# Differential attention in a two-layer hybrid backbone: the order of a head pair's key and query projections, and which engine takes which reciprocal root

## The chip, the cores and the metric

The kernel runs on one core of one Trainium2 chip. The metric is the device time of one execution in microseconds (us). Before the change the median of three runs is 1973.07 us (1971.86 to 1974.28); smaller is better.

## What is computed

Two layers of a diffusion backbone work on 256 latent tokens and 256 context tokens, 1024 channels each, in float32. In each layer one input projection feeds three mixers (a recurrence in both directions, latent attention with 16 heads, differential attention with 8 heads); their merged output and a SwiGLU block are added to the stream. The last layer computes outputs, and so queries, for the 256 latent tokens alone. What matters here is the differential attention:

```python
def _rmsnorm(x, g):
    y = xf * lax.rsqrt(jnp.mean(xf * xf, axis=-1, keepdims=True) + EPS)
    return (y * g.astype(jnp.float32)).astype(x.dtype)

def _diff_qk(t, g, rope):                      # queries and keys alike
    u = jnp.moveaxis(t.reshape(B, T, DIFF_HEADS, 2, DIFF_HD), 3, 2)   # two maps of 64 per head
    u = _rmsnorm(u, g)
    return _apply_rope(u, *rope) if rope is not None else u

# in _layer; _attention: out = sum_m mix_w[m] * softmax(scale * q_m k_m^T) v
kd_l, kd_c = _diff_qk(dk, diff_k_g, rope_diff), _diff_qk(dkc, diff_k_g, None)
o_c = _attention(_diff_qk(dq, diff_q_g, rope_diff), concat(kd_l, kd_c), concat(vd_l, vd_c), [1, -lam], DIFF_SCALE)
```

## The kernel before

Arithmetic at float32 precision is made of three passes of a split product: each operand is held as a high and a low half (`split`, L136 to 141), and `mm3` (L199) multiplies high by high, low by high and high by low. Weights arrive as blocks of 128 x 1024 (`wload`, L156): one DMA on SyncE, then ScalarE rounds the high half (`wh`, or `room` for two more buffers in the second layer), and VectorE subtracts it to get the low half (`wl` or `room`). The ring has three blocks in the first layer and five in the second.

**The differential attention** goes through its 8 heads in pairs. `diff_proj(hp)` (L891) is a generator that projects one pair: queries (tiles `ddq`), keys (`ddk`) and values (`dvH`, `dvL`). Each projection is one `gemm_tm` (L449) over two weight blocks; `pst` is its PSUM tile, two token tiles of 128 to a bank. Keys and values always take four token tiles, 96 matmuls of 256 columns; queries take four in the first layer (96 matmuls) and two in the last (48). When two token tiles are ready, `qk_tm` (L892) squares them on ScalarE (`scr`, L894), and on VectorE rotates the latent ones (`rope_tm`, L603: L606, two L610, L616) or multiplies the context ones by the gain (L902), and sums the squares (L904).

**The reciprocal roots** of those sums come from `rsqrt` (L204): three small VectorE operations for a first guess (L210, L213, L214), then three Newton steps. With `soon=True` the steps are nine VectorE operations (L217 to L219), without it twelve GpSimd operations (L222 to L225), one behind the other:

```python
        if soon:
            for _ in range(3):
                V.scalar_tensor_tensor(out=t, in0=y, scalar=-0.5, in1=y, op0=ALU.mult, op1=ALU.mult)
                ...
            return y
        for _ in range(3):
            G.tensor_tensor(out=t, in0=y, in1=y, op=ALU.mult)
            ...
```

Before the change the queries' roots (`drq`) are made on GpSimd and the keys' (`drk`) on VectorE. Keys are multiplied by their root in place (L922, four operations). Queries never are: their root is the scale of the softmax's exponential, and a VectorE operation of one column (L622) and ScalarE's exponential (L623) read `drq`.

**Around it.** `diff_prep(h)` (L934) transposes the head's keys (`dtrk`, L939) and then its queries (`dtrq`, L944) on TensorE and splits them. `diff_sc(h)` computes the two score maps of each query tile in one pair of banks (`S`, L663) and the softmax. `diff_pv(h)` multiplies by the values (`po`, 12 matmuls), transposes the result (`subt`, L992), squares it on ScalarE (L996), takes its root on VectorE (`subr`, again L212 to L219) and scales it (L1000, which reads `subt`). `diff_sub(h)` transposes it back (L1007).

**Two PSUM banks** (`ps_tr`, L95, `bufs=2`) serve all transposes in turn. In the loop over the heads (L1140) a new pair's `dtrq` follows the `subt` of an earlier head by two places, so it takes the bank that L1000 reads.

**What sets the order.** Projections are put on a queue and `fill(ns)` draws matmuls from it between the steps of the attention; `need(hp, dk_)` (L929) draws until the pair is entered in the dictionary `dk_`:

```python
            def need(hp, d):
                while hp not in d:
                    credit[0] = 0.0
                    fill(1)
```

A scheduler then orders each engine's instructions by its own estimate of when they are ready and by priority, the order of the code for most; weight splits go ahead by 90. Every engine runs its instructions strictly in that order.

Of the kernel before, what the change touches and what calls it, by code (L numbers as in the profile page):

```python
# [28 lines left out]
EPS = 1e-6  # L29
# [5 lines left out]
RQ, RK, RDQ, RDK = 0, 32, 64, 128  # L35
NROW = 192

W_RX, W_RG, W_MG, W_DQ, W_DK, W_DV, W_BA, W_BB, W_BC, W_OUT, W_G, W_U = 0, 4, 8, 20, 24, 28, 32, 36, 40, 44, 48, 59
# [25 lines left out]
def tile_hybrid(ctx: ExitStack, tc: tile.TileContext, xt, cvec, cwide, prm, row, dlam, rope, wmod, wmod0, wmodt, wfm, wcq, wckv, wuq, wukv, wlru, wfo, out):  # L64
# [91 lines left out]
    def wload(src, n=1024, now=True):  # L156

        if now and ready:
            key, H, L = ready.popleft()
            assert key == str(src)  # L160
            return H, L
        st = stage()
        nc.sync.dma_start(st[:, :n], src)
        ring["w"] = (ring["w"] + 1) % (WB + len(more["w"]))
        if ring["w"] < WB:
            H = wp.tile([P, 1024], F32R, tag="wh", name="wh")
            L = wp.tile([P, 1024], F32R, tag="wl", name="wl")
        else:
            H, L = more["w"][ring["w"] - WB]
        tc.cur_priority -= first_by[0]  # L170
        parts = split(H[:, :n], L[:, :n], st[:, :n])
        for b, a in zip(parts, hold):
            issue_after(b, a)
        hold.clear()
        low[0] = parts[1]
        tc.cur_priority += first_by[0]
        pace[1] += pace[0]
        while pace[1] >= 1:
            pace[1] -= 1
            slow_step(1)  # L180
        return H, L
# [17 lines left out]
    def mm3(ps, wH, wL, xH, xL, start, stop, skip=False):  # L199
        nc.tensor.matmul(ps, wH, xH, start=start, stop=False, skip_group_check=skip)  # L200
        nc.tensor.matmul(ps, wH, xL, start=False, stop=False, skip_group_check=skip)  # L201
        nc.tensor.matmul(ps, wL, xH, start=False, stop=stop, skip_group_check=skip)  # L202

    def rsqrt(ss, scale, eps, n, name, add=None, soon=False):  # L204

        v = sm.tile([P, n], F32, tag="rqv", name=name + "v", bufs=2)
        t = sm.tile([P, n], F32, tag="rqt", name=name + "t", bufs=2)
        y = sm.tile([P, n], F32, tag="rqy", name=name, bufs=8)
        if add is None:
            V.tensor_scalar(out=v, in0=ss, scalar1=scale, scalar2=eps, op0=ALU.mult, op1=ALU.add)  # L210
        else:
            V.scalar_tensor_tensor(out=v, in0=ss, scalar=scale, in1=add, op0=ALU.mult, op1=ALU.add)  # L212
        V.tensor_scalar(out=y.bitcast(I32), in0=v.bitcast(I32), scalar1=1, scalar2=None, op0=ALU.logical_shift_right)  # L213
        V.tensor_scalar(out=y.bitcast(I32), in0=y.bitcast(I32), scalar1=-1, scalar2=0x5F3759DF, op0=ALU.mult, op1=ALU.add)  # L214
# [3 lines that stand above are left out]
                V.tensor_tensor(out=t, in0=t, in1=v, op=ALU.mult)  # L218
                V.scalar_tensor_tensor(out=y, in0=t, scalar=1.5, in1=y, op0=ALU.add, op1=ALU.mult)  # L219
# [3 lines that stand above are left out]
            G.tensor_tensor(out=t, in0=t, in1=v, op=ALU.mult)  # L223
            G.tensor_scalar(out=t, in0=t, scalar1=-0.5, scalar2=1.5, op0=ALU.mult, op1=ALU.add)
            G.tensor_tensor(out=y, in0=y, in1=t, op=ALU.mult)  # L225
        return y
# [29 lines left out]
    def mm_ns(n):  # L256
        return n / 2.4 + 2.5
# [191 lines left out]
    def gemm_tm(l, widx, xH, xL, toks, ps_, consume):  # L449

        pss = [ps_(f"pst{i}").rearrange("p (t n) -> p t n", t=2) for i in range(len(toks) // 2)]
        for hf in range(2):
            H, L = wload(wfm[l, widx, hf])
            H = H.rearrange("p (k n) -> p k n", n=256)
            L = L.rearrange("p (k n) -> p k n", n=256)
            for i, tt in enumerate(toks):
                for kk in range(4):
                    k = hf * 4 + kk
                    mm3(pss[i // 2][:, i % 2, :], xH[:, k, tt * P:(tt + 1) * P], xL[:, k, tt * P:(tt + 1) * P], H[:, kk, :], L[:, kk, :], k == 0 and i % 2 == 0, k == KT - 1 and i % 2 == 1, True)
                if hf == 1 and i % 2 == 1:  # L460
                    consume(toks[i - 1], pss[i // 2])
                yield 12 * mm_ns(256)
# [80 lines left out]
    for l in range(LAYERS):  # L543
        last = l == LAYERS - 1
        TQ = SEQ if last else T
        qtoks = [0, 1] if last else [0, 1, 2, 3]
        nq = len(qtoks)
# [3 lines left out]
        with ExitStack() as c1:  # L551
# [7 lines left out]
            def t_tok(name):  # L559
                return tk.tile([P, 384], F32, tag="tok", name=name, bufs=8)  # L560
# [7 lines left out]
            def t_v(name, dt=F32R):  # L568
                return tmp("v", 6, dt=dt, name=name)
# [7 lines left out]
            def t_sc():  # L577
                return tmp("sc", 2, name="scr")

            if l == 0:  # L580
# [8 lines left out]
                hH = big.tile([P, KT, T], F32R, tag="big", name="hH")  # L589
                hL = big.tile([P, KT, T], F32R, tag="big", name="hL")  # L590
# [298 lines left out]
            dq_, dk_, drq, dvv, dqk, dpr, dpt, dsub, ds0 = {}, {}, {}, {}, {}, {}, {}, {}, {}  # L889

            def diff_proj(hp):  # L891
                def qk_tm(tt0, ps, ss, store, key, ro):  # L892
                    scr = t_sc()
                    A.activation(scr, ps.rearrange("p t c -> p (t c)"), AF.Square)  # L894
                    for i in range(2):
                        u = t_tok("d" + key)
                        uv = u[:, :256].rearrange("p (h d) -> p h d", d=64)
                        sv_ = ps[:, i, :].rearrange("p (h d) -> p h d", d=64)
                        if tt0 == 0:
                            rope_tm(uv, sv_, tabs[key], i, 4, 64)  # L900
                        else:
                            V.tensor_tensor(out=uv, in0=sv_, in1=rw[:, ro:ro + 64].unsqueeze(1).to_broadcast([P, 4, 64]), op=ALU.mult)  # L902
                        store[tt0 + i] = u
                    V.tensor_reduce(out=ss[:, tt0:tt0 + 2, :], in_=scr.rearrange("p (t h d) -> p t h d", t=2, d=64), axis=AX.X, op=ALU.add)  # L904

                def v_tm(tt0, ps):
                    for hh in range(2):
                        d = [w_[:, tt0 * P:(tt0 + 2) * P].rearrange("p (t c) -> p t c", t=2) for w_ in vv[hh]]
                        split(d[0], d[1], ps[:, :, hh * P:(hh + 1) * P])

                ssq = sm.tile([P, 4, 4], F32, tag="ssq", name="dssq", bufs=2)
                ssk = sm.tile([P, 4, 4], F32, tag="dssk", name="dssk", bufs=2)
                qd, kd = {}, {}
                yield from gemm_tm(l, W_DQ + hp, hH, hL, qtoks, ps_mm, lambda tt0, ps: qk_tm(tt0, ps, ssq, qd, "dq", RDQ))
                rq = rsqrt(ssq[:, :nq, :].rearrange("p a b -> p (a b)"), 1.0, 64 * EPS, nq * 4, "drq")
                drq[hp] = rq.rearrange("p (a b) -> p a b", b=4)
                yield from gemm_tm(l, W_DK + hp, hH, hL, alltoks, ps_mm, lambda tt0, ps: qk_tm(tt0, ps, ssk, kd, "dk", RDK))
                rk = rsqrt(ssk.rearrange("p a b -> p (a b)"), 1.0 / 64, EPS, 16, "drk", soon=True).rearrange("p (a b) -> p a b", b=4)
                yield 1
                for tt in range(4):  # L920
                    uv = kd[tt][:, :256].rearrange("p (h d) -> p h d", d=64)
                    V.tensor_tensor(out=uv, in0=uv, in1=rk[:, tt, :].unsqueeze(2).to_broadcast([P, 4, 64]), op=ALU.mult)  # L922
                dq_[hp], dk_[hp] = qd, kd
                yield 1
                vv = [(t_v("dvH"), t_v("dvL")) for _ in range(2)]
                dvv[hp] = vv
                yield from gemm_tm(l, W_DV + hp, hH, hL, alltoks, ps_mm, v_tm)
# [205 lines left out]
            three_banks(f"pair{l}")  # L1133
            singles[0] = 1
            queue.append(diff_proj(0))
            need(0, dk_)
            run(gemm_fm(l, W_BB, 2, oH, oL, TQ, ps_mm, proj_acc))
# [25 lines left out]
            rk = c1.enter_context(tc.tile_pool(name=f"rk{l}", bufs=1, reuse_waits="tile"))  # L1163
# [112 lines left out]
        with ExitStack() as c1:  # L1276
# [73 lines left out]
            for q in range(2):  # L1350
# [37 lines left out]
                hH = big.tile([P, KT, T], F32R, tag="big", name="hH")  # L1388
                hL = big.tile([P, KT, T], F32R, tag="big", name="hL")
# [106 lines left out]
```

## Time and profile before

| | us |
|---|---|
| three runs, median (lowest to highest) | 1973.07 (1971.86 to 1974.28) |
| the profiled execution, as timed | 1974.12 |
| its span, first to last instruction | 1972.3 |
| TensorE (PE) busy in it | 1930.2 (98%) |
| VectorE (DVE) busy | 1568.3 (80%) |
| ScalarE (ACT) busy | 1069.9 (54%) |
| GpSimd (POOL) busy | 58.8 (3%) |

Rows name a line of the kernel, an engine, and the tile written and read. PEld is TensorE's weight load, which runs beside PE; both wait in TensorE's one stream. In a row of the timeline stand its start in us from the span's start, its length, and in brackets the idle time of its engine just ahead of it with what ended that. Differential attention of the first layer lies between about 258 and 530 us, that of the second between about 1362 and 1600 us. The granted clock of TensorE is at full speed in all of it.

### The profile page before, as it was taken

How to read it: one execution, taken by the hardware profiler on the slowest of the kernel's cores; microseconds unless marked ns; L12 is line 12 of the kernel's file. 1: busy time of each engine (PE TensorE's matmuls, PEld its weight loads, DVE VectorE, ACT ScalarE, POOL GpSimd, SP SyncE). 2: the span in 40 equal slices, each digit the busy share in tenths (PEclk: the TensorE clock that was granted, in tenths of full speed). 3: DMA queues.
4: the chain of work that ended last, by engine and by line, in shares of the span. 5: the costliest groups of instructions: out<-in, count | busy, mean ns of one | idle time of the engine just before them, and what ended most of it. 6: DMA issues, size and time to landing. Idle time of an engine off the chain costs nothing. (4 is left out here: it accounts for less than half of the span.)

```text
span 1972.3 us, 31832 instructions
## 1 busy us (share of the span) xinstructions
PE 1930.2 (98%) x11746; PEld 1666.3 (84%) x11746; DVE 1568.3 (80%) x3838; ACT 1069.9 (54%) x1975; POOL 58.8 (3%) x198
## 2 busy tenths in 40 slices
PE   7999999999999999999999999999999999899999
PEld 4888888988678878888888888988999788898888
DVE  5679965788798888789888876898688889966763
ACT  4568833455576663353233224798444678845552
POOL 0001000000000000000000000012010000000000
PEclk9999999999999999999999999999999999999999
DMA  8311122212234456536656653422322234474553
GB/s 291 99 41 51 53 65 77 76 55 67 70 102 129 140 191 197 184 127 201 196 191 201 200 176 115 151 64 76 128 93 80 65 123 143 156 231 150 185 189 108
DMA packets 91068, 258.16 MB, mean 131 GB/s; under 512 B 10144, under 2 KB 17312, under 8 KB 90656
## 3 DMA queue, kind: packets, MB, share of 16 engines
q1 hardware_dynamic: 90912, 256.13, 39.8%
q8 instruction: 92, 1.51, 0.3%
q14 instruction: 64, 0.52, 0.1%
HBM read 250.85 MB, written 5.24 MB: 130 GB/s over the span
## 5 line engine op out<-in xcount | busy, mean ns | idle before, releaser
L138 ACT ACTIVATE wh<-st 128x1024 fp32r<-128x1024 f32 (+4 forms) x305 | 308.4, 1012 | 367.8 <-PE ps L201 173.1
L138 DVE TENSOR_TENSOR wl<-st,wh 128x1024 fp32r<-128x1024 f32 (+4 forms) x305 | 354.2, 1162 | 125.5 <-ACT wh L138 122.0
L200 PE MATMUL ps<-hH,wh 128*128 128x512 f32 (+1 forms) x504 | 182.0, 361 | 3.8 <-ACT gt L1118 2.9
L202 PE MATMUL ps<-hH,wl 128*128 128x512 f32 (+1 forms) x504 | 180.6, 359 | 1.7 <-DVE wl L138 1.7
L201 PE MATMUL ps<-hL,wh 128*128 128x512 f32 (+1 forms) x504 | 181.3, 360 | 0.0
L200 PE MATMUL pst<-wh,hH 128*128 128x256 f32 x568 | 164.3, 289 | 0.0
L201 PE MATMUL pst<-wl,hH 128*128 128x256 f32 x568 | 162.1, 285 | 0.0
L202 PE MATMUL pst<-wh,hL 128*128 128x256 f32 x568 | 161.9, 285 | 0.0
L200 PE MATMUL ps<-h2H,wh 128*128 128x512 f32 (+1 forms) x368 | 139.1, 381 | 0.7 <-ACT h2H L379 0.7
L201 PE MATMUL ps<-h2L,wh 128*128 128x512 f32 (+1 forms) x368 | 139.5, 380 | 0.0
L202 PE MATMUL ps<-h2H,wl 128*128 128x512 f32 (+1 forms) x368 | 139.5, 380 | 0.0
L621 DVE TENSOR_REDUCE st<-S 128x1 f32<-128x512 f32 (+1 forms) x192 | 113.0, 596 | 21.4 <-ACT dp L623 11.2
L138 DVE TENSOR_TENSOR room<-acc,room 128x1024 fp32r<-128x1024 f32 (+3 forms) x75 | 87.6, 1169 | 30.6 <-ACT room L138 29.1
L200 PEld LDWEIGHTS pst<-wh,hH 128*128 128x128 f32 x568 | 108.6, 191 | 3.8 <-issue 3.3
L200 PEld LDWEIGHTS ps<-hH,wh 128*128 128x128 f32 x504 | 95.3, 189 | 19.3 <-ACT gt L1118 3.9
L202 PEld LDWEIGHTS pst<-wh,hL 128*128 128x128 f32 x568 | 108.5, 191 | 1.7 <-issue 1.4
L201 PEld LDWEIGHTS pst<-wl,hH 128*128 128x128 f32 x568 | 108.6, 191 | 1.1 <-issue 0.7
L202 PEld LDWEIGHTS ps<-hH,wl 128*128 128x128 f32 x504 | 95.2, 189 | 15.6 <-DVE wl L138 2.3
L310 DVE SCALAR_TENSOR_TENSOR ms<-ms,cb 128x512 f32<-128x512 f32 x160 | 107.3, 688 | 1.3
L138 ACT ACTIVATE room<-acc 128x1024 fp32r<-128x1024 f32 (+3 forms) x75 | 76.2, 1017 | 57.6 <-PE ps L201 20.5
L201 PEld LDWEIGHTS ps<-hL,wh 128*128 128x128 f32 x504 | 95.3, 189 | 12.8
L310 DVE SCALAR_TENSOR_TENSOR sq<-ms,cb 128x512 f32<-128x512 f32 x112 | 75.7, 689 | 31.9 <-DMA ms<-wmodt 31.0
(585 smaller groups left out, 5558.3 us busy)
## 6 DMA issues: line engine op xcount, KB each, us to landing
st<-wfm SPq DMA_DIRECT2D x224, 512.0 KB, 3.5
ms<-wmodt SPq DMA_DIRECT2D x160, 256.0 KB, 2.8
acc<-wfm SPq DMA_DIRECT2D x56, 512.0 KB, 3.5
st<-wfo SPq DMA_DIRECT2D x35, 512.0 KB, 3.5
mstage<-wmod SPq DMA_DIRECT2D x16, 512.0 KB, 5.3
acc<-wfo SPq DMA_DIRECT2D x9, 512.0 KB, 3.5
st<-wlru SPq DMA_DIRECT2D x7, 512.0 KB, 3.4
st<-wukv SPq DMA_DIRECT2D x13, 256.0 KB, 2.6
```

The source lines that it names most:

```text
L138: return A.activation(dH, src, AF.Copy), V.tensor_tensor(out=dL, in0=src, in1=f(dH), op=ALU.subtract)
L200: nc.tensor.matmul(ps, wH, xH, start=start, stop=False, skip_group_check=skip)
L201: nc.tensor.matmul(ps, wH, xL, start=False, stop=False, skip_group_check=skip)
L202: nc.tensor.matmul(ps, wL, xH, start=False, stop=stop, skip_group_check=skip)
L310: issue_after(V.scalar_tensor_tensor(out=o, in0=st, scalar=1.0, in1=cb[:, v, :], op0=ALU.mult, op1=ALU.mult, accum_out=sums[:, i - i0, h, ...
L621: V.tensor_reduce(out=st[:, 0:1], in_=S, axis=AX.X, op=ALU.max, negate=True)
```

## The change

Inside `diff_proj` the keys' projection, their root and their multiplication now come first, and the queries' projection and root after them. The keys' root loses `soon=True` and is made on GpSimd; the queries' root gets it and is made on VectorE. The pair is entered in `dq_` and `dk_` after the queries' root, with no `yield` behind it, so that `need` returns only when the first token tile of the values' projection has been issued too. L922 of before is L919 of after.

```diff
                 qd, kd = {}, {}
-                yield from gemm_tm(l, W_DQ + hp, hH, hL, qtoks, ps_mm, lambda tt0, ps: qk_tm(tt0, ps, ssq, qd, "dq", RDQ))
-                rq = rsqrt(ssq[:, :nq, :].rearrange("p a b -> p (a b)"), 1.0, 64 * EPS, nq * 4, "drq")
-                drq[hp] = rq.rearrange("p (a b) -> p a b", b=4)
                 yield from gemm_tm(l, W_DK + hp, hH, hL, alltoks, ps_mm, lambda tt0, ps: qk_tm(tt0, ps, ssk, kd, "dk", RDK))
-                rk = rsqrt(ssk.rearrange("p a b -> p (a b)"), 1.0 / 64, EPS, 16, "drk", soon=True).rearrange("p (a b) -> p a b", b=4)
+                rk = rsqrt(ssk.rearrange("p a b -> p (a b)"), 1.0 / 64, EPS, 16, "drk").rearrange("p (a b) -> p a b", b=4)
                 yield 1
                 for tt in range(4):
                     uv = kd[tt][:, :256].rearrange("p (h d) -> p h d", d=64)
                     V.tensor_tensor(out=uv, in0=uv, in1=rk[:, tt, :].unsqueeze(2).to_broadcast([P, 4, 64]), op=ALU.mult)
+                yield 1
+                yield from gemm_tm(l, W_DQ + hp, hH, hL, qtoks, ps_mm, lambda tt0, ps: qk_tm(tt0, ps, ssq, qd, "dq", RDQ))
+                rq = rsqrt(ssq[:, :nq, :].rearrange("p a b -> p (a b)"), 1.0, 64 * EPS, nq * 4, "drq", soon=True)
+                drq[hp] = rq.rearrange("p (a b) -> p a b", b=4)
                 dq_[hp], dk_[hp] = qd, kd
-                yield 1
                 vv = [(t_v("dvH"), t_v("dvL")) for _ in range(2)]
```

How it moves instructions is shown at two places of the second layer. The first is VectorE at the third head pair (hp = 2), where the last projection of the pair has just ended. Before, the keys' chain and the chain of `subr` run in step, the keys are multiplied, and L1000 follows:

```order
L138 TENSOR_TENSOR room<-acc,room 128x1024 [waits DMAHW6_49,Activation_49]
L210 TENSOR_SCALAR drkv<-dssk 128x16 [waits DVE_49]
L212 SCALAR_TENSOR_TENSOR subrv<-subss,s_16013 128x2 [waits Activation_49,Pool_49]
L213 TENSOR_SCALAR drk<-drkv 128x16 [waits DVE_49]
...
L922 TENSOR_TENSOR ddk<-ddk,drk 128x256 [waits DVE_49]
L922 TENSOR_TENSOR ddk<-ddk,drk 128x256 x3
L1000 TENSOR_TENSOR so<-subt,subr 128x256 [waits DVE_49,PE_49]
```

After, at the same place of VectorE's stream:

```order
L213 TENSOR_SCALAR drk<-drkv 128x16 [waits DVE_49]
L606 TENSOR_TENSOR ddq<-pst_16391,tabdq 128x256 [waits Activation_49]
L214 TENSOR_SCALAR drk<-drk 128x16 [waits DVE_49]
L610 TENSOR_TENSOR rp<-pst_16391,tabdq 128x128 x2
L606 TENSOR_TENSOR ddq<-pst_16391,tabdq 128x256
L616 TENSOR_TENSOR ddq<-ddq,rp 128x256 [waits DVE_49]
L904 TENSOR_REDUCE dssq<-scr 128x8
L919 TENSOR_TENSOR ddk<-ddk,drk 128x256 [waits Pool_49]
L919 TENSOR_TENSOR ddk<-ddk,drk 128x256 x3
...
L212 SCALAR_TENSOR_TENSOR subrv<-subss,s_16013 128x2 [waits Activation_49]
...
L1000 TENSOR_TENSOR so<-subt,subr 128x256 [waits DVE_49,PE_49]
```

L214, the last VectorE step ahead of the GpSimd chain, now stands behind the first rotation of the queries; the keys' multiplication waits for GpSimd (Pool) with only four rows between; and the queries' second rotation, one weight split, both chains and L1000 stand behind it.

The same place on TensorE, the transposes for the first head of that pair (`pst_16519` and `pst_16480` are the values' tile before and after). Before:

```order
L939 MATMUL dtrk<-ident,ddk 128x128 [waits DVE_49] x4
L944 MATMUL dtrq<-ident,ddq 128x128 [waits DVE_49,Activation_49]
L944 MATMUL dtrq<-ident,ddq 128x128
L663 MATMUL S<-dkH,dqH 128x512 x2
L200 MATMUL pst_16519<-wh,hH 128x256
```

After:

```order
L939 MATMUL dtrk<-ident,ddk 128x128 [waits DVE_49] x4
L663 MATMUL S<-dkH,dqH 128x512 x2
L663 MATMUL S<-dkL,dqH 128x512 x2
L663 MATMUL S<-dkH,dqL 128x512 x2
L944 MATMUL dtrq<-ident,ddq 128x128 [waits DVE_49,Activation_49]
L944 MATMUL dtrq<-ident,ddq 128x128
L200 MATMUL pst_16480<-wh,hH 128x256
```

The score matmuls moved ahead of `dtrq`; between the end of the pair's last projection and `dtrk` stand 48 matmuls of values, 12 of `po` and 2 of `subt` both before and after.

The second place is VectorE at the second head pair (hp = 1) of the second layer. Before:

```order
L922 TENSOR_TENSOR ddk<-ddk,drk 128x256 [waits DVE_49]
L922 TENSOR_TENSOR ddk<-ddk,drk 128x256 x3
L138 TENSOR_TENSOR room<-acc,room 128x1024 [waits DMAHW1_49,Activation_49]
L621 TENSOR_REDUCE st_16023<-S 128x1 [waits PE_49]
L138 TENSOR_TENSOR dkL<-dtrk,dkH 128x512 [waits Activation_49]
```

After:

```order
L138 TENSOR_TENSOR wl<-st,wh 128x1024 [waits DMAHW7_49,Activation_49]
L919 TENSOR_TENSOR ddk<-ddk,drk 128x256 [waits Pool_49]
L919 TENSOR_TENSOR ddk<-ddk,drk 128x256 x3
L606 TENSOR_TENSOR ddq<-pst_15834,tabdq 128x256 [waits Activation_49]
...
L138 TENSOR_TENSOR room<-acc,room 128x1024 [waits DMAHW0_49,Activation_49]
L616 TENSOR_TENSOR ddq<-ddq,rp 128x256 [waits DVE_49]
```

The queries' rotations now stand behind the wait for GpSimd, and their last step (L616) behind one more weight split; on TensorE, `dtrk` and `dtrq` come directly behind the 48 matmuls of values here, ahead of the score matmuls.

## Rows read from the trace of the kernel before

**Rows 1.** The page's first part: busy time, share, instructions.
```profile
PE 1930.2 (98%) x11746; PEld 1666.3 (84%) x11746; DVE 1568.3 (80%) x3838; ACT 1069.9 (54%) x1975; POOL 58.8 (3%) x198
```

**Rows 2.** Waits of PEld and PE, whole span: total us, times, longest.
```profile
PEld S L663 <- ACT dp L623: 8.5, 27, 0.7
PEld dtrk L939 <- DVE ddk L922: 2.8, 10, 0.5
...
PE dtrq L944 <- DVE so L1000: 0.4, 1, 0.4
```

**Rows 3.** Timeline of POOL, queries' root of hp 1, first layer.
```profile
351.46 0.21 POOL L222 TENSOR_TENSOR drqt<-drq 128x16 f32<-128x16 f32 x1 [83.04 <-DVE drq L214]
...
352.65 0.22 POOL L222 TENSOR_TENSOR drqt<-drq 128x16 f32<-128x16 f32 x1
...
354.73 1.13 POOL L225 TENSOR_TENSOR drq<-drq,drqt 128x16 f32<-128x16 f32 x1
```

**Rows 4.** Timeline of DVE at the same place.
```profile
354.56 1.22 DVE L138 TENSOR_TENSOR wl<-st,wh 128x1024 fp32r<-128x1024 f32 x1 [3.24 <-ACT wh L138]
```

**Rows 5.** Timeline of PE, hp 2 of the second layer, from the keys' end.
```profile
1480.27 0.28 PE L985 MATMUL po<-pH,dvH 128*128 128x256 f32 x1
...
1481.59 0.28 PE L987 MATMUL po<-pH,dvL 128*128 128x256 f32 x1
...
1487.94 0.60 PE L939 MATMUL dtrk<-ident,ddk 128*128 128x128 f32 x4
1488.38 0.38 PE L944 MATMUL dtrq<-ident,ddq 128*128 128x128 f32 x2
```

**Rows 6.** Timeline of ACT at the same place.
```profile
1480.53 0.60 ACT L894 ACTIVATE scr<-pst 128x512 f32<-128x512 f32 x1 [2.34 <-PE pst L202]
```

**Rows 7.** Timeline of DVE at the same place.
```profile
1480.22 0.48 DVE L610 TENSOR_TENSOR rp<-pst,tabdk 128x128 f32<-128x128 f32 x2
1480.73 0.43 DVE L616 TENSOR_TENSOR ddk<-ddk,rp 128x256 f32<-128x256 f32 x1
...
1482.43 1.21 DVE L138 TENSOR_TENSOR room<-acc,room 128x1024 fp32r<-128x1024 f32 x1
...
1486.08 1.43 DVE L922 TENSOR_TENSOR ddk<-ddk,drk 128x256 f32<-128x256 f32 x4
1487.43 0.42 DVE L1000 TENSOR_TENSOR so<-subt,subr 128x256 f32<-128x256 f32 x1
```

**Rows 8.** Timelines of PE and DVE, hp 3 of the second layer.
```profile
1521.85 0.28 PE L985 MATMUL po<-pH,dvH 128*128 128x256 f32 x1
...
1529.01 0.42 DVE L1000 TENSOR_TENSOR so<-subt,subr 128x256 f32<-128x256 f32 x1
```

**Rows 9.** Timeline of DVE, hp 1 of the second layer.
```profile
1430.44 0.42 DVE L606 TENSOR_TENSOR ddq<-pst,tabdq 128x256 f32<-128x256 f32 x1 [1.20 <-ACT scr L894]
...
1434.04 0.42 DVE L616 TENSOR_TENSOR ddq<-ddq,rp 128x256 f32<-128x256 f32 x1
...
1444.82 0.17 DVE L214 TENSOR_SCALAR drk<-drk 128x16 int32<-128x16 int32 x1
...
1446.91 1.43 DVE L922 TENSOR_TENSOR ddk<-ddk,drk 128x256 f32<-128x256 f32 x4
```

**Rows 10.** Timeline of PE, hp 1 of the second layer.
```profile
1446.98 0.50 PE L663 MATMUL S<-dkH,dqH 64*128 64x512 f32 x2
...
1447.87 0.85 PE L939 MATMUL dtrk<-ident,ddk 128*128 128x128 f32 x4
```

**Rows 11.** Timelines of PE and DVE, hp 3 of the first layer.
```profile
466.55 0.66 PE L992 MATMUL subt<-ident,so 128*128 128x128 f32 x4
...
468.55 0.16 DVE L212 SCALAR_TENSOR_TENSOR subrv<-subss,s 128x4 f32<-128x4 f32 x1 [0.75 <-ACT scr L996]
...
472.60 0.69 DVE L1000 TENSOR_TENSOR so<-subt,subr 128x512 f32<-128x512 f32 x1
...
473.43 0.63 PE L944 MATMUL dtrq<-ident,ddq 128*128 128x128 f32 x4 [0.36 <-DVE so L1000]
```

## The prediction, made before the changed kernel had run

> **What bounds the kernel now.** I read the page's first part first: TensorE is busy for 98% of the span [rows 1], so a change that takes no matmul away and adds none can move the time only through the few per cent in which TensorE stands. The change adds and removes no matmul. Next I read the waits of TensorE's two streams. Two kinds belong to the edited steps: the key transposes wait for the keys' multiplication, 2.8 us in ten places, and one query transpose waits 0.4 us for L1000, which still reads the bank that it wants [rows 2]. The largest kind in the attention, the score matmuls that wait for the exponential ahead of them, is 8.5 us in 27 places [rows 2]. So there are about 3.2 us that the edit can win where it works, and no reserve: whatever makes TensorE stand longer goes into the time nearly whole. Last I read the timelines around the eight head pairs, because VectorE obeys its order strictly and a new wait in its stream delays all that is queued behind.
>
> **What the change removes.** The keys' nine Newton steps on VectorE leave the way from the last key to its transposes, and the four multiplications move ahead of the queries' projection. With that the 2.8 us of waiting for the keys go, and the 0.4 us for L1000 is counted anew below: 3.2 us gained at most. VectorE's own work stays: the queries get the nine steps, with 16 columns in the first layer as the keys had, 8 in the last.
>
> **What it adds: a wait of VectorE for GpSimd, eight times.** The chain on GpSimd has twelve operations. Undisturbed, four of them take 1.19 us (352.65 less 351.46 [rows 3]), so twelve take 3.57 us. The multiplication L919 waits for the last of them, and everything behind it on VectorE waits too. What does that cost? It depends on the place.
>
> At hp 0 and hp 1 of the first layer nothing else is due: VectorE stood idle for 3.24 us at this very spot before [rows 4], and the queries' projection, 96 matmuls, runs meanwhile. I cost these two and hp 0 of the second layer, whose transposes come only after a long projection of another branch, at nothing. If that cover were gone, each would cost 3.57 us.
>
> At hp 2 of the second layer I follow the new order. TensorE issues a 256-column matmul each 0.12 us (eleven steps of `po` in 1.32 us [rows 5]). The pair's last projection ends at the same time as before, about 1480.27 us by the old trace, for the work ahead of it is the same. ScalarE squares that result until 1481.13 [rows 6]; only then may VectorE begin the queries' rotation L606 (0.42 [rows 9]), and L214 (0.17 [rows 9]) stands behind it: 1481.65. Now GpSimd starts. Some operations of VectorE that run beside it read tiles in SBUF as it does, and one such overlap cost dearly before: an operation of GpSimd took 1.13 us against 0.22 while VectorE subtracted a weight half [rows 3, 4]. So the chain lasts from 3.57 us (no overlap) to 4.5 (one such overlap). I take 4.0, between them, as the operations of VectorE that now run beside it are shorter than that weight split: 1485.65. The four L919 occupy 1.35 us until the next start (1487.43 less 1486.08 [rows 7]): 1487.0. The rest of the rotation takes 0.94 (1480.22 to the end of L616 [rows 7]): 1487.95. One weight split and the two small chains took 3.65 us from 1482.43 to 1486.08 [rows 7], of which some 0.2 now run earlier: 1491.4. L1000 takes 0.42 [rows 7]: 1491.8.
>
> When is TensorE there? Before, `dtrk` began at 1487.94 and `dtrq` 0.44 us later [rows 5]. The work ahead of `dtrk` is the same, and it finds its keys ready (1487.0); but the six score matmuls, 0.89 us (1446.98 to 1447.87 [rows 10]), now stand between it and `dtrq`: 1489.3. `dtrq` takes the bank that L1000 reads, so TensorE stands from 1489.3 to 1491.8, **2.5 us** (2.1 to 3.0 with the chain's bounds). Before, L1000 was done at 1487.85, half a microsecond ahead of `dtrq`. At hp 3 the rows repeat to the hundredth (L1000 starts 7.16 us behind the first `po` in both [rows 5, 7, 8]) and the new order is alike: again **2.5**.
>
> The Trainium skill, page "SBUF — State Buffer", section "Who interferes with whom", says that a VectorE instruction with two SBUF inputs and a GpSimd instruction that reads SBUF exclude each other for a whole instruction. By that rule only L616 of the four rows between L214 and L919 (0.43 us in the row above) would hold the chain, so 4.0 us is its ceiling there and 2.5 us the wait's; the rows 3 and 4 show one such exclusion, and its length fits (1.13 us until the weight split's end), but no row shows which operations do not exclude.
>
> At hp 1 of the second layer there is no L1000 in the way; the queries themselves come late. The last projection ends 48 matmuls (5.76 us) ahead of 1446.98 [rows 10], at 1441.22, and the keys' now another 5.76 us earlier, 1435.46. L214 ended 3.77 us after the keys [rows 9, 10]: 1439.23. The chain ends at 1442.8, or at 1443.7 with one overlap, since a weight split now stands between L214 and L919. L919: 1444.2 or 1445.1. The queries' rotation with its weight split took 4.02 us (1430.44 to 1434.46 [rows 9]): 1448.2 or 1449.1. TensorE wants the second `dtrq` at about 1447.4 (1446.98 and the 0.44 of `dtrk`). It stands for 0.8 to 1.7 us; I take **1.3**.
>
> At hp 2 and hp 3 of the first layer the queries have 96 matmuls, so the keys' wait is over early. But `need` now lets 12 matmuls of values go ahead of `po`, and these are missing between `subt` and `dtrq`: 18 remain (2.16 us), with `subt` and `dtrk` (0.44 each) and the scores (0.89) about 4.0 us. VectorE needs 2.0 us from `subt` to `subrv` (466.55 to 468.55), fourteen small operations, nine of which each follow on the last at 0.21 us (ten in 2.09 us [rows 9]), about 2.4 together, and L1000 with 0.69 [rows 11]: 5.1. That makes 1.0 us of standing each; 2.2 if the keys' wait has pushed the queries' rotation back by 1.2 us, my estimate of what remains of the chain's 3.57 when VectorE has done the softmax steps between L214 and L919. I take **1.4** each. The new order has more independent work beside the keys' transposes of hp 1, which I leave at nothing.
>
> **The sum.** 2.5 + 2.5 + 1.3 + 1.4 + 1.4 = 9.1 us added, 3.2 taken: **+5.9 us**. The profiled execution, 1974.12 us (span 1972.3 and 1.8 around it), would become 1980.0; it lies 1.05 us above the median, so the median becomes 1979.0. Lower bound: 2.1 + 2.1 + 0.8 + 1.0 + 1.0 less 3.2 is +3.8, 1976.9. Upper bound: 3.0 + 3.0 + 1.7 + 2.2 + 2.2 and nothing gained is +12.1, 1985.2. A measurement here can tell about 0.2%, 3.9 us, from no change.
>
> **Rivals.** *The standing is paid back* (not slower): while TensorE waits at `dtrq`, ScalarE and VectorE get through the softmax, and the score matmuls behind find their banks free. For it speaks that 8.5 us of such waits exist [rows 2]; against it, that it is VectorE that is late, and it comes out of the wait with the same queue. It decides if over half of the 9.1 us return: 9.1 less 4.3 (half of the 8.5) less 3.2 is +1.6, 1974.7, within 0.2%. Chance 0.27.
>
> *The waits for GpSimd hide everywhere* (faster): if the two banks were not claimed as I read, or TensorE reached `dtrq` later, only the 3.2 us and some of the score waits (a quarter, 2.1) would count: -5.3, 1967.8. For it speaks that three of eight places are idle on VectorE; against it, the 0.4 us for L1000, which shows the bank's claim [rows 2, 11]. Chance 0.09.
>
> *The wait reaches the weights too* (slower still): weight splits are queued behind L919. If at each of the five busy places TensorE also stood for what is left of the chain, 3.57 less the 2 us of rows between, 1.6 each, the sum would be 5.9 + 8 = +13.9, 1987.0. Against it: the ring holds three or five blocks, and a block feeds 2.9 to 5.8 us of matmuls. Chance 0.04.
>
> That the change does not do what it says is not among them: the order shows the keys ahead and L919 waiting for Pool at all eight places.
>
> **How the numbers follow.** The forecast, slower by 3.8 to 12.1 us, has 0.60; with the third rival 0.04. Slower by over 0.2%: 0.64; within: 0.27; faster: 0.09. The likeliest time is 1979.0. The range runs from 1972.0, which leaves out the faster case and a fifth of the paid-back one (its own range is 1970 to 1977), to 1985.5, the upper bound: about 0.18 is left out. The forecast's own range is 1976.9 to 1985.2.
>
> **What would show it.** In the profile after, VectorE's waits must name `ddk` L919 behind GpSimd, some 8 times and 15 us or more in total; TensorE's must name `dtrq` behind `so` L1000, 2 to 3 us at each of two places of the second layer, and about 1 at two of the first; waits of `dtrk` for `ddk` must be gone. GpSimd's chain at hp 2 and 3 of the second layer should begin near 1481.8 and 1523.4. I am wrong if `dtrq` finds its bank free, if the score waits fall by as much as `dtrq` adds, or if TensorE's busy share rises.

## The result, and the profile after

The changed kernel takes 1990.24 us (median of four runs, 1989.12 to 1993.48) against 1973.25 us before: a ratio of 1.0087, 95% interval 1.0075 to 1.0099. It is slower by some 17 us, where 5.9 were forecast and 12.1 was the upper bound.

The page's first part, after (the answer to [rows 1]; the span is 1987.9 us, before 1972.3):

```profile
PE 1934.4 (97%) x11746; PEld 1671.2 (84%) x11746; DVE 1571.6 (79%) x3838; ACT 1070.8 (54%) x1975; POOL 53.5 (3%) x198
```

TensorE ran the same 11746 matmuls. Its busy time rose by 4.2 us, so that some of them ran slower, and its idle time (span less busy) rose from 42.1 to 53.5 us, by 11.4. Together that is the 15.6 us by which the span grew. So there are two losses, and only one of them was in the forecast.

Waits after, whole span (engine, what it waited for, total us, times, longest), which answer to [rows 2]:

```profile
DVE ddk L919 <- POOL drk L225: 20.7, 8, 3.7
...
PEld S L663 <- ACT dp L623: 10.2, 27, 2.1
PE dtrq L944 <- DVE so L1000: 9.9, 4, 2.9
...
PE dtrq L944 <- DVE ddq L616: 1.7, 1, 1.7
```

VectorE waits for GpSimd at eight places. TensorE waits for L1000 at four and for the queries (L616) at one, 11.6 us in all. The key transposes no longer wait for `ddk`. The place in the second layer that was followed step by step (hp = 2), first VectorE, then GpSimd, then TensorE (timelines; compare [rows 5, 7]):

```profile
1492.46 0.17 DVE L214 TENSOR_SCALAR drk<-drk 128x16 int32<-128x16 int32 x1
...
1493.27 0.41 DVE L616 TENSOR_TENSOR ddq<-ddq,rp 128x256 f32<-128x256 f32 x1
...
1496.46 1.43 DVE L919 TENSOR_TENSOR ddk<-ddk,drk 128x256 f32<-128x256 f32 x4 [2.18 <-POOL drk L225]
...
1502.10 0.42 DVE L1000 TENSOR_TENSOR so<-subt,subr 128x256 f32<-128x256 f32 x1
```

```profile
1492.71 0.21 POOL L222 TENSOR_TENSOR drkt<-drk 128x16 f32<-128x16 f32 x1 [41.20 <-DVE drk L214]
...
1493.31 0.43 POOL L224 TENSOR_SCALAR drkt<-drkt 128x16 f32<-128x16 f32 x1
...
1496.20 0.22 POOL L225 TENSOR_TENSOR drk<-drk,drkt 128x16 f32<-128x16 f32 x1
```

```profile
1498.87 0.60 PE L939 MATMUL dtrk<-ident,ddk 128*128 128x128 f32 x4
...
1499.96 0.39 PE L663 MATMUL S<-dkH,dqL 64*128 64x512 f32 x2
1502.67 0.41 PE L944 MATMUL dtrq<-ident,ddq 128*128 128x128 f32 x2 [2.32 <-DVE so L1000]
```

The chain on GpSimd lasts 3.71 us (1492.71 to 1496.42), VectorE stands for 2.18 of it, the rest of the queries' rotation, a weight split, both chains and L1000 come only behind that, and TensorE stands for 2.32 us. All of that is the forecast's mechanism. What the forecast did not have is in the next table: TensorE's granted clock in the first layer at hp = 2 (window, its length, then busy us and instructions of PE, PEld, DVE, ACT and POOL, the granted clock as a share of full speed, and two DMA columns):

```profile
416.00:420.00 4.00, 2.21 (x16) 1.43 (x14) 3.41 (x23) 0.60 (x1) 0.00 (x0) 0.97 0.39 131
420.00:424.00 4.00, 3.48 (x17) 3.51 (x17) 2.77 (x6) 1.67 (x3) 0.00 (x0) 0.50 0.01 2
424.00:428.00 4.00, 4.00 (x26) 4.00 (x26) 2.85 (x6) 3.01 (x7) 0.00 (x0) 0.68 0.00 0
428.00:432.00 4.00, 4.00 (x33) 3.46 (x32) 3.23 (x9) 1.20 (x4) 0.00 (x0) 1.00 0.38 134
```

TensorE stood for 2.3 us up to 420.5. The granted clock then fell to half, 1.2 of 2.4 GHz: in the window from 420, in half a microsecond of which TensorE still stood, 17 matmuls went through, and in the one from 428, at full speed, 33. The transposes there show it in one row (compare [rows 11], the same transposes at hp = 3 before, 0.63 us):

```profile
420.52 1.09 PE L944 MATMUL dtrq<-ident,ddq 128*128 128x128 f32 x4 [2.30 <-DVE so L1000]
```

Such falls stand at four places of the attention after (from about 420, 536, 1457 and 1546 us) and at none before. One window of each of the other three:

```profile
536.00:540.00 4.00, 4.00 (x12) 3.08 (x12) 1.93 (x7) 2.45 (x6) 0.00 (x0) 0.60 0.28 105
1456.00:1460.00 4.00, 3.05 (x13) 2.18 (x14) 3.69 (x15) 0.70 (x2) 0.00 (x0) 0.68 0.41 131
1544.00:1548.00 4.00, 1.67 (x9) 1.50 (x8) 3.90 (x22) 0.84 (x2) 0.00 (x0) 0.77 0.36 131
```

Busy time times the missing share of the clock, summed over windows of 4 us, makes 7.3 us of them; at the end of the kernel, where both kernels have two falls, it is 2.9 against 4.2. The windows show one execution, but the mean granted clock of every run agrees: 0.993 to 0.995 in the four runs of the changed kernel, 0.995 to 0.998 in 53 runs of the kernel before.

### The profile page after: what moved, and what is told of

The parts are those of the page before. It is cut to its first block, busy times and chain, and to the rows that moved or that the text cites. A ratio compares the mean times of both kernels' runs of the same rounds, so it can differ in the third digit from the quotient of the medians.

```text
span 1987.9 us, 31830 instructions
## 1 busy us (share of the span) xinstructions
PE 1934.4 (97%) x11746; PEld 1671.2 (84%) x11746; DVE 1571.6 (79%) x3838; ACT 1070.8 (54%) x1975; POOL 53.5 (3%) x198
## 4 chain that ended last, share of the span: by engine, by line
PE 62%; DVE 12%; ACT 6%; issue 3%; POOL 1%; DMA 0%; POOLq 0%; DVEq 0%; ACTq 0%
PE ps L200 11%; PE ps L201 10%; PE ps L202 10%; PE ps L428 4%; PE po L202 2%; PE po L201 2%; PE po L200 2%; PE pst L200 2%; PE pst L202 2%; PE pst L201 2%; PE ps L429 2%; DVE wl L138 2%; PE ptr L635 2%; PE po L1365 1%; PE S L663 1%
## 5 line engine op out<-in xcount | busy, mean ns | idle before, releaser
L138 ACT ACTIVATE wh<-st 128x1024 fp32r<-128x1024 f32 (+4 forms) x305 | 308.3, 1013 | 360.5 <-PE ps L201 180.5
L138 DVE TENSOR_TENSOR wl<-st,wh 128x1024 fp32r<-128x1024 f32 (+4 forms) x305 | 354.2, 1163 | 122.5 <-ACT wh L138 119.1
L200 PE MATMUL pst<-wh,hH 128*128 128x256 f32 x624 | 181.9, 291 | 0.0
L201 PE MATMUL pst<-wl,hH 128*128 128x256 f32 x624 | 180.0, 289 | 0.0
L202 PE MATMUL pst<-wh,hL 128*128 128x256 f32 x624 | 179.8, 288 | 0.0
L621 DVE TENSOR_REDUCE st<-S 128x1 f32<-128x512 f32 (+1 forms) x192 | 113.0, 597 | 25.4 <-ACT dp L623 14.4
L200 PEld LDWEIGHTS pst<-wh,hH 128*128 128x128 f32 x624 | 120.9, 194 | 3.5 <-issue 3.1
L201 PEld LDWEIGHTS pst<-wl,hH 128*128 128x128 f32 x624 | 120.8, 194 | 2.8 <-issue 2.2
L202 PEld LDWEIGHTS pst<-wh,hL 128*128 128x128 f32 x624 | 120.7, 193 | 2.0 <-issue 1.8
L138 DVE TENSOR_TENSOR room<-acc,room 128x1024 fp32r<-128x1024 f32 (+3 forms) x75 | 87.5, 1168 | 29.3 <-ACT room L138 27.9
L138 ACT ACTIVATE room<-acc 128x1024 fp32r<-128x1024 f32 (+3 forms) x75 | 76.2, 1017 | 59.8 <-PE ps L201 19.4
L623 ACT ACTIVATE dp<-S,st,drq 128x512 f32<-128x512 f32 (+1 forms) x96 | 67.7, 705 | 57.4 <-DVE st L622 37.0
```

Of the source, the lines that this page charges most:

```text
L138: return A.activation(dH, src, AF.Copy), V.tensor_tensor(out=dL, in0=src, in1=f(dH), op=ALU.subtract)
L621: V.tensor_reduce(out=st[:, 0:1], in_=S, axis=AX.X, op=ALU.max, negate=True)
L623: A.activation(dst, S, AF.Exp, scale=sc_ap, bias=st[:, 1:2], accum_out=st[:, 2:3] if total is None else total)
```

## Experiments

Theory A: VectorE's wait for GpSimd makes VectorE late, and TensorE stands for it at `dtrq`. Theory B: the new order of the projections does it. Ratios are against runs of the kernel before that were taken together with the run.

**The order alone.** The new order, both roots on the engines of before:

```diff
-                rk = rsqrt(..., 16, "drk")...
+                rk = rsqrt(..., 16, "drk", soon=True)...
...
-                rq = rsqrt(..., nq * 4, "drq", soon=True)
+                rq = rsqrt(..., nq * 4, "drq")
```

> The new order of the projections, but both reciprocal roots on the engines of before: the keys' on VectorE, the queries' on GpSimd. Theory A (VectorE's wait for GpSimd holds L1000, and TensorE stands at dtrq behind it): the waits of L919 for GpSimd are gone, dtrq waits for so L1000 under 2 us in all instead of 9.9, the granted clock does not fall in the differential attention, and the time is 1968 to 1978 us. Theory B (the order alone does it: queries projected last and twelve matmuls of values drawn ahead make dtrq come before VectorE is done): dtrq still stands 7 us or more in all, 1985 to 1992 us.

Measured: 1975.62 us, ratio 1.0007 (0.9997 to 1.0016). The waits for GpSimd are gone, `dtrq` waits 2.2 us for L1000 (A had put under 2), all of it in the first layer, and the clock does not fall in the attention. The order alone costs nothing that can be measured.

**The engines alone.** The old order with the roots swapped (`soon=True` moved from the keys' root to the queries').

> The old order of the projections, but the roots swapped: keys' on GpSimd, queries' on VectorE. Theory A: the chain of 3.6 us now lies directly between the last keys and their transposes, and VectorE has the chain of subr (about 1.9 us) beside it; VectorE waits some 1.5 to 2 us for GpSimd at each busy place, dtrk waits about 1.5 to 2 us longer for ddk at each of five or six places: 1979 to 1987 us. Theory B: without the new order no more than 2 us are lost, 1972 to 1976 us.

Measured: 1990.03 us, ratio 1.0082 (1.0066 to 1.0097), as slow as the whole change and above what A expected. Here TensorE stands at the key transposes, and the clock fell in the attention too (4.2 us by the same sum). Waits, whole span:

```profile
DVE ddk L922 <- POOL drk L225: 22.1, 8, 3.7
PEld dtrk L939 <- DVE ddk L922: 12.2, 21, 2.4
```

So the loss comes with the engines, in either order, and shows where TensorE next needs VectorE. That speaks for A and against B.

**How long GpSimd takes.** The keys' root with one Newton step, and with six (`steps=1` or `6` in the loop over L222 to L225, for `drk` alone; with one step the root is only a rough one). At the four places where TensorE stood for L1000, its order between `dtrk` and `dtrq` is that of the changed kernel to within one matmul.

> The changed kernel with one Newton step instead of three in the keys' root on GpSimd (four operations, 1.2 us); the keys' root is then only a rough one, as two steps are left out. Theory A: VectorE has other rows for longer than that between L214 and L919 at the busy places, so it waits at most 5 us in all; dtrq waits for so L1000 0 to 3 us in all, the clock does not fall, 1972 to 1979 us. Rival E: over 1985 us.

> The changed kernel with six Newton steps instead of three in the keys' root on GpSimd (24 operations, some 7.1 us; the value is the same to rounding). Theory A: VectorE's wait for GpSimd grows by 3.6 us at each of eight places, to some 49 us; TensorE's standing grows by about 3.6 at each of five places, 18 us, and the clock falls behind each: 2006 to 2016 us. Rival E (the loss is one of order and clock, and hardly depends on the chain's length): under 1998 us.

Measured: 1975.40 us (ratio 1.0003, 0.9994 to 1.0013) and 2014.38 us (1.0196, 1.0181 to 1.0211). With one, three and six steps VectorE waits:

```profile
DVE ddk L919 <- POOL drk L225: 6.6, 8, 1.4
```

```profile
DVE ddk L919 <- POOL drk L225: 43.7, 8, 7.3
```

and 20.7 us between them; A had put at most 5 us with one step and some 49 with six. The loss follows the length of the chain: (1990.24 - 1975.40) / (20.7 - 6.6) and (2014.38 - 1990.24) / (43.7 - 20.7) are each 1.05 us of time for each microsecond that VectorE waits, the clock's part and the harmless places included. The changed kernel was timed apart from the other two; by the ratios the rates are 1.2 and 0.9, so about one. With one step the clock does not fall in the attention, with six it falls at five places there, worth 13.9 us.

**Both roots on VectorE**, in the new order (`soon=True` for the keys too).

> The new order with both roots on VectorE. No operation of VectorE waits for GpSimd in the differential attention; VectorE has nine small operations more for each pair than with the keys' or the queries' root on GpSimd, about 1.9 us. Theory A (what counts is how late VectorE comes to L1000, whatever makes it late): about as late as with the wait of 2.2 us, so dtrq waits for so L1000 6 to 10 us in all and the time is 1983 to 1990 us. Rival D (only the standing wait for another engine costs, since VectorE's own operations are fitted in between): 1974 to 1979 us.

Measured: 1973.14 us, ratio 0.9992 (0.9983 to 1.0002), a little less than D expected. Here A as I had put it was wrong: VectorE has more to do than in the changed kernel (1577.1 us busy against 1571.6), and nothing is lost. The timeline of VectorE at hp = 2 of the second layer shows one reason:

```profile
1481.95 0.17 DVE L217 SCALAR_TENSOR_TENSOR drkt<-drk 128x16 f32<-128x16 f32 x1
1482.04 0.28 DVE L610 TENSOR_TENSOR rp<-pst,tabdq 128x128 f32<-128x128 f32 x1
1482.24 0.17 DVE L218 TENSOR_TENSOR drkt<-drkt,drkv 128x16 f32<-128x16 f32 x1
1482.32 0.28 DVE L610 TENSOR_TENSOR rp<-pst,tabdq 128x128 f32<-128x128 f32 x1
```

Between independent rows a step of the chain takes 0.08 to 0.09 us from start to start. I had counted 0.2 us each, as they take one behind the other. Nine of them cost about 0.8 us, where the wait for GpSimd costs 2.2 at the same place. It also tells that the queries' root on VectorE is not the loss, which leaves the keys' root on GpSimd.

There is a second reason at that place: TensorE's order is not that of the changed kernel. Twelve matmuls of values stand between the scores and `dtrq`, and `dtrq` waits for `dkL`, which reads `dtrk`, and not for L1000, which begins behind it (so it does not take the bank that L1000 reads there):

```profile
1491.72 0.44 PE L944 MATMUL dtrq<-ident,ddq 128*128 128x128 f32 x2 [0.24 <-DVE dkL L138]
...
1492.24 0.42 DVE L1000 TENSOR_TENSOR so<-subt,subr 128x256 f32<-128x256 f32 x1
```

L1000 is even later here than in the changed kernel, 11.5 us behind the end of the pair's last projection (1480.73) against 10.9, and no longer matters. The order and the bank are like that at hp = 3 too, and in the run of the order alone, with eleven matmuls. So in the second layer these two runs change what TensorE asks for as well as what VectorE does, and they do not tell the two apart. In the first layer TensorE's order between `dtrk` and `dtrq` is the same to within one matmul; there `dtrq` waits for L1000 0.75 us at each of two places instead of 2.30 and 2.91. The run with one step, where that order stays in both layers, is the cleaner one.

**Another bank.** `subt` in the single bank of `po` (`ps_sc("subt")`), in the changed kernel and in the kernel before, so that `dtrq` takes no bank that L1000 reads.

> The changed kernel, with the tile subt in the single bank of po in place of the two banks of the transposes, so that dtrq no longer takes a bank that L1000 reads. VectorE still waits for GpSimd about 20 us in all. Theory A: dtrq waits for so L1000 nowhere, the 9.9 us and the falls of the clock behind them go: 1974 to 1981 us. Rival C (VectorE is late, and TensorE meets that at the next tile instead: dtrq behind ddq, the scores behind dqL, po behind L1000): 1985 us or more, with the 9.9 us under other names.

> The kernel before with subt in the bank of po. It tells what the bank is worth without the change. Theory A: only the 0.4 us that dtrq waited for L1000 can go, 1970 to 1975 us. Rival C (po now waits for L1000 of the head before): over 1977 us.

Measured: 1995.37 us (ratio 1.0109, 1.0094 to 1.0124) and 1983.55 us (1.0051, 1.0034 to 1.0068). The other bank costs 8 us by itself, among them 4.3 us that TensorE waits for L1000 ahead of the transposes back. The change still costs 11.8 us on top of it. `dtrq` waits for L1000 nowhere; TensorE's waits have other names:

```profile
PE ptr L635 <- DVE dkL L138: 11.0, 9, 2.4
...
PE dtrq L944 <- DVE ddq L616: 1.7, 1, 1.7
```

A was wrong here and rival C right: the bank is where the lateness shows, and not what makes most of it cost.

**Work drawn ahead**: 24 or 36 matmuls of the projections between `dtrk` and `dtrq` of each new pair.

```diff
                 split(kH, kL, ptk)
+                if h in (2, 4, 6):
+                    fill(3600)
                 ptq = ps_tr("dtrq")
```

> The changed kernel with 24 or 36 matmuls of the projections drawn from the queue between the key and the query transposes of the first head of each new pair (they are taken from later places, none is added). VectorE's wait for GpSimd stays about 20 us. Theory F (TensorE's order has too little work ahead of dtrq for the time that VectorE is late, and that is all of the loss, with the clock behind it): dtrq waits for so L1000 under 2 us in all, the clock does not fall there, 1972 to 1979 us. Rival C (the lateness only shows at the next tile, since the work drawn ahead is missing later): 1984 us or more.

Measured: 1990.38 us, ratio 1.0083 (1.0067 to 1.0099): nothing is won, against theory F. `dtrq` no longer waits for L1000, but other waits of TensorE grow by about as much, and the clock still falls at two places (from about 410 and 471 us, 2.8 us):

```profile
PE S L663 <- ACT dp L623: 9.8, 9, 2.8
PE ptr L635 <- DVE dkL L138: 4.9, 3, 2.4
```

The first was 2.7 us in the changed kernel. Matmuls that fill one gap were missing in the next.

**Filler**: 28 matmuls that nothing reads, ahead of `dtrk` at the five places where TensorE stood.

```diff
                 ptk = ps_tr("dtrk")
+                if h in ((4, 6), (2, 4, 6))[l]:
+                    for _ in range(28):
+                        nc.tensor.matmul(ptk[:, :256], hH[:, 0, :P], hH[:, 0, :256], start=True, stop=True, ...)
```

> The changed kernel with 28 matmuls of 256 columns that nothing reads, put ahead of the key transposes at the five places where TensorE stood: 140 of them, 16.8 us of added work at full speed, in place of 11.6 us of standing. Theory G (the clock fell because TensorE stood): the standing and the four falls of the clock (7.9 us) go: 1990.2 + 16.8 - 11.6 - 7.9 = 1987.5, so 1985 to 1990 us, and the granted clock is 1.0 throughout the attention. Rival H (the clock falls there whether TensorE stands or not): 1993 to 1997 us.

Measured: 1987.81 us, ratio 1.0072 (1.0056 to 1.0088), 16.8 us of added work and yet no slower than the change; the mean granted clock of its four runs is 0.996 to 0.998, as before the change. VectorE waits 20.0 us for GpSimd as before, but where the clock had fallen it is full (windows, same columns):

```profile
420.00:424.00 4.00, 3.84 (x30) 2.88 (x29) 3.14 (x6) 2.47 (x4) 0.00 (x0) 1.00 0.00 2
...
1544.00:1548.00 4.00, 3.70 (x31) 3.06 (x30) 3.60 (x7) 1.82 (x4) 0.00 (x0) 1.00 0.49 157
```

In the changed kernel these two windows are at 0.50 and 0.77. Three of the four falls are gone, those at the places that were filled, so there the clock fell because TensorE stood. The one near 536 us stays (1.6 us), where G had none; a wait of 2.1 us for the gate (`gt` L1121), at no filled place, stands ahead of it.

**The yield put back** behind the entry of the pair, in the changed kernel and in the two orders without the wait for GpSimd:

```diff
                 dq_[hp], dk_[hp] = qd, kd
+                yield 1
```

> The changed kernel with the yield behind the entry of the pair put back, so that the twelve matmuls of values stay between subt and dtrq in the first layer. Theory A with the term for twelve matmuls (1.44 us) as predicted: dtrq's wait for so L1000 in the first layer falls from 5.2 to about 2.3 us, the second layer's 4.6 stays, and the time is 1984 to 1989 us. Rival: the twelve matmuls do not matter, 1989 to 1992 us.

> The new order with the roots on the engines of before (keys' on VectorE, queries' on GpSimd) and the yield put back. Theory F: the 2.2 us that dtrq waited for L1000 in the first layer go: 1969 to 1974 us. Rival: no difference from the order without the yield, 1974 to 1977 us.

> The new order with both roots on VectorE and the yield put back behind the entry of the pair, so that twelve matmuls stay between subt and dtrq in the first layer. Theory F: what dtrq still waited there (1.5 us) goes, and nothing else changes: 1968 to 1973 us. Rival: VectorE's nine more operations for each pair show elsewhere: 1975 us or more.

Measured: 1982.77 us (ratio 1.0044, 1.0031 to 1.0056), 1970.25 us (0.9983, 0.9974 to 0.9993) and 1970.61 us (0.9985, 0.9975 to 0.9995). In the first, `dtrq` waits 2.0 us for L1000 in the first layer instead of 5.2, and of the clock's 4.7 us in that layer 1.3 are left: the missing `yield` was worth some 8 us of the change (7.5 by the times, 8.5 by the ratios), more than expected, since falls of the clock went with the waits. Its eight runs lie between 1980.51 and 1988.31 us, with mean granted clocks from 0.997 down to 0.994, and the trace is of the fastest: how far the clock falls differs from run to run. The two others are faster than the kernel before, by some 3.3 us, about the 3.2 that the forecast had as the gain: keys ahead of queries do help, with the `yield` kept and the keys' root on VectorE.

## Why the prediction was wrong, point by point

**Right.** The direction, the cause and the places. The key transposes no longer wait for `ddk`, VectorE waits for GpSimd at eight places (20.7 us, 15 or more forecast), and at hp 0 and hp 1 of the first layer its waits of 3.7 us are followed by no wait of TensorE. The second layer's three terms were 2.5, 2.5 and 1.3 us; they measure 2.32, 2.33 and 1.66. The steps at hp 2 hold as well: counted from the end of the pair's last projection (1491.24 in the new trace), GpSimd begins after 1.5 us where 1.4 were forecast, TensorE comes to `dtrq` after 9.1 (9.0), and L1000 ends after 11.3 (11.5). The chain's length was put at 4.0 us with 3.57 and 4.5 as bounds and is 3.71 there. The rule of the Trainium skill ("SBUF — State Buffer", section "Who interferes with whom") agrees with these rows: beside L616 (two SBUF inputs, 0.41 us) one GpSimd operation takes 0.43 us in place of 0.20 and ends 0.06 us behind it, and the other eleven are as short as ever.

**Wrong: the sum had no term for the clock.** This is the step that failed. I took each microsecond that TensorE stands as one microsecond lost. Behind four waits in the attention the granted clock fell to half and stayed there for 3 to 6 us, 7.3 us of loss. The section on what bounds the kernel read TensorE's waits but not what a longer one does to the matmuls behind it. Without the clock the measured waits less the gain, 11.6 - 3.2 = 8.4 us, lie inside the forecast's 3.8 to 12.1. The filler shows the cause at three of the four places, 5.7 of the 7.3 us.

**Wrong in size: hp 2 and hp 3 of the first layer**, 1.4 us each, 2.2 at most; they measure 2.30 and 2.91. The base of that term held: it was 1.0 us, and without any wait for GpSimd (the order alone) the two places measure 1.09 and 1.10, with 0.57 us of it (one step) 1.14 and 1.00. Mis-sized is what the wait for GpSimd adds. I put it at 1.2 us at most and took 0.4; VectorE waits 1.86 and 2.19 us there, and `dtrq` waits 1.2 and 1.8 us longer than with the order alone. The lateness shows between `subt` and `subrv`, for which I took the 2.0 us of [rows 11]. After the change nine of the twelve rows of the queries' chain stand ahead of `subrv`, 0.21 us apiece, and VectorE begins them 1.7 us behind `subt`, where with one step it is 0.1:

```profile
415.46 0.17 DVE L210 TENSOR_SCALAR drqv<-dssq 128x16 f32<-128x16 f32 x1
...
416.08 0.18 DVE L217 SCALAR_TENSOR_TENSOR drqt<-drq 128x16 f32<-128x16 f32 x1
416.29 0.17 DVE L218 TENSOR_TENSOR drqt<-drqt,drqv 128x16 f32<-128x16 f32 x1
...
417.22 0.15 DVE L212 SCALAR_TENSOR_TENSOR subrv<-subss,s 128x4 f32<-128x4 f32 x1
```

`subt` began at 413.75, so 3.5 us passed, and 3.75 at hp 3 (472.22 to 475.97); with one step it is 2.3 and 2.1. The order showed these rows; I had priced the queries' chain as work that stays and not asked what it now stands ahead of. Both places need two things together: the wait for GpSimd and the twelve missing matmuls. Without the one `dtrq` waits 2.2 us for L1000 there, without the other 2.0, with both 5.2.

**The sum again, with what was measured:** waits at `dtrq` 11.6 us in place of 9.1, less the 3.2 gained, plus 7.3 for the clock in the attention, less 1.3 for the clock at the end: 14.4 us, against 15.6 in the span, so 1.2 us are left without a name. It also fits the two losses of the profile: PE's own waits at `dtrk` and `dtrq` for these two causes rose from 0.6 us to 11.6, 11.0 of the 11.4 by which its idle time grew; the clock makes 6.0 us of busy time, less the other 2.6 of the gain if that had counted as busy before, 3.4 of 4.2. For that reading speaks that four key transposes at hp 3 of the first layer take 1.34 us before (471.73) and 0.60 after (474.86).

**The rivals.** Nothing was paid back: waits of the score matmuls rose from 8.5 us to 10.2 instead of falling. They are not a loss of their own: PE's wait of 2.17 us for the gate (L1118) near 530 us before is gone, and one of 1.68 us for an exponential stands near 534 after. Drawing work ahead, the way in which the standing could have been paid back, won nothing either. The weights were not reached: PE's waits for a low weight half (L138) are 7.2 us before and 7.3 after.

**Open.** Why two waits of the same length (2.91 us at 479.27 and 2.32 us at 1502.67) were not followed by a fall of the clock is not known. Nor does any run tie the fall near 536 us, 1.6 of the 7.3, to the wait for GpSimd. In the changed kernel it stands behind the wait of 1.68 us for an exponential; the order alone has the same wait, of the same length (528.37), and the kernel before has the one of 2.17 us for the gate (530.52), and neither has a fall there.

## What to carry to other kernels

A step moved to an idle engine is not taken off the busy one if the busy one waits for the answer in a strict order: ask how much of its own work stands between the hand-over and the wait, and compare that wait with what the step costs among independent rows (here 2.2 us against 0.8). When TensorE is the bound, price a new wait of it not by its length alone: take as the upper bound the wait and the matmuls behind it at half the clock (here for 3 to 6 us). Before taking away the place where a wait shows (a bank, an order), change the length of what is waited for, and see whether the order around it stayed: that told the cause here, and the bank and the order did not.

## What the runs showed of the hardware

- The granted clock of TensorE fell to half (1.2 GHz) behind four waits of 1.66 to 2.33 us, and was back at full speed 3 to 6 us after it fell, with TensorE at work (420.5 to 426.5, 535.9 to 539.2); behind two others of 2.32 and 2.91 us it stayed at 2.4 GHz.
- Small VectorE operations (128x16, float32) that each need the last one follow at 0.21 us; with an independent row between them they add 0.08 to 0.09 us each.
- In the keys' chains of the changed kernel one GpSimd operation took 1.21 us (1391.50) and one 1.22 us in place of 0.22, both times beside a weight split of 1.23 us on VectorE. The second is at hp 1 of the second layer and is the one overlap for which the forecast had 1.7 us there:

```profile
1447.23 1.23 DVE L138 TENSOR_TENSOR wl<-st,wh 128x1024 fp32r<-128x1024 f32 x1 [0.35 <-ACT wh L138]
```

```profile
1447.32 1.22 POOL L223 TENSOR_TENSOR drkt<-drkt,drkv 128x16 f32<-128x16 f32 x1
```
